# One-core HGRN2, stick-breaking attention and PEER experts: how the experts' input is repeated, and which block moves are transposes

## The chip, the cores and the metric

The kernel runs on one core of one Trainium2 chip. The time is device microseconds of one execution. Of the kernel before there are three runs, 3661.49, 3661.97 and 3666.92 us, median 3661.97, and one more execution under the profiler, which took 3659.19 us.

## The reference, cut to what matters

A model of two layers over 1024 tokens of 1024 features, all in float32. Layer 0 mixes tokens with HGRN2, layer 1 with stick-breaking attention; each layer then has a PEER stage, in which every token reads 64 experts out of 16384.

```python
# layer l: mix, then experts
hn = modulate(rms_norm(h, norm_mix_g[l]), sh1, sc1)
mix = hgrn2_mixer(...) if l == 0 else stick_breaking_mixer(...)
h = h + g1 * mix
hn = modulate(rms_norm(h, norm_ffn_g[l]), sh2, sc2)
h = h + g2 * peer_ffn(hn, ...)

# stick-breaking attention, per query block: a key counts only if it is earlier
mask = s_pos < t_pos
log_keep = where(mask, log_sigmoid(-z), 0)
a = where(mask, exp(z + cs_in + after), 0)      # then a @ v

# experts, per token: 4 heads x 16 best of 128 x 128 keys
hid = einsum('cd,ced->ce', x, u[experts])
w = gates * gelu(hid)
out = einsum('ce,ced->cd', w, v[experts])
```

## The kernel before, in words

**Blocks and stages.** The 1024 tokens are eight blocks of 128. Layer 0's mixer runs on three groups of blocks (`G0`: 0-1, 2-4, 5-7), `hgrn_group`, each followed by its routing (`mix_route`), which finds the 64 experts of each token. Layer 1's attention runs on two groups (`G1`: 0-3, 4-7), `attn_group`, each followed by `route_group`. The attention of a group needs layer 0 finished for the group's blocks, and the experts of a block need its routing. So the expert stage of one set of blocks runs beside the mixer of the next.

**The expert stage.** Each row of a table holds an expert's `u` and `v` (2048 floats). A block is worked off in four quarters of 32 tokens (`peer_quarter`). A quarter's 32 tokens stand on the 128 partitions four times, one copy per head, so that one gather (`L690`, an indirect DMA issued by GpSimd, 128 rows of 8 KB, 1 MB) brings one expert for each token and head, and 16 gathers make a quarter. VectorE multiplies the `u` half with the tokens' input `hq` and sums along the row (`L692`), ScalarE takes gelu of the sums of two gathers (`L694`) and scales a small selection matrix with them (`L696`, tile `sel`), and TensorE adds up the `v` halves, weighted, in PSUM (`L699`, tile `va`; four matmuls per gather, each two instructions in the profile, since a float32 matmul is made of two). The gather tile `g` has six buffers; a buffer is free once L699 has read it.

**The experts' input.** `peer_input` makes the block's normed and modulated tokens `hn2` (128 x 1024, one buffer). Its modulation rows come from columns: `row_bcast` (`L183`) multiplies a column, repeated 128 times as the stationary operand, with the identity, which gives the column as a row on all partitions. `peer_rep` repeats a quarter: two matmuls (`L666`) with a 0/1 matrix `rep4` take the 32 partitions of the quarter in `hn2` to four places, in two halves of 512 columns through one PSUM bank (tag `pq`, one buffer), and ScalarE copies each half to `hq` (`L667`, two buffers). It also makes `dg` (`L669`), the gates on diagonals, with `delta`, a part of `rep4`.

**Other block moves.** `norm_T` (`L266`) turns normed token blocks so that features stand on partitions, by matmul with the identity, or with the reversed identity `anti` where attention wants the keys in reverse. `norm_heads` (`L423`) makes rows of the head norms as `row_bcast` does. Two places already use TensorE's transpose mode: `L502` and `L783`.

**The attention head.** `attn_head` multiplies queries and keys into PSUM, up to four key blocks at a time (`L770`); for the diagonal block a second matmul (`L772`) adds `amask`, -1e30 where the key is not earlier. ScalarE takes tanh (`L773`, tile `th`), VectorE forms the stick-breaking weights with a running product (`L774` to `L777`), TensorE turns them (`L783`), ScalarE copies them (`L784`), TensorE multiplies with the values (`L786`).

**What sets the order.** The Tile framework orders the instructions of each engine when the kernel is built, by a list scheduler with its own estimates of durations. `at(t)` gives what follows a due time: the gathers of block b in layer l are due at `T0 + PERIOD * (8l + b + i/64) - LEAD`, a quarter's repeat (`peer_rep`) 20 before its first gather, which is about six gathers, and the first quarter's 60. Each engine then works off its queue in that fixed order, waiting by semaphores.

Of the kernel before, what the change touches and what calls it, by code (L numbers as in the profile page):

```python
# [10 lines left out]
F32 = mybir.dt.float32  # L11
BF16 = mybir.dt.bfloat16
I32 = mybir.dt.int32
U32 = mybir.dt.uint32
AF = mybir.ActivationFunctionType
ALU = mybir.AluOpType
# [6 lines left out]
GH, GMAX = 3, 4  # L23
# [2 lines left out]
FREE = 1  # L26
LEAD, RLEAD = 100, 60
NC = 2
BIG = -1e30
NEG = -3.0e38  # L30

T0, PERIOD = 305.0, 207.0
# [5 lines left out]
def tile_model(ctx, tc, x, cin, small, ada, w_in, w_out, kvada, kvw, sbq, sbo, wq, subk, tab0, tab1, out):  # L38
    nc = tc.nc
    V, S, G, T = nc.vector, nc.scalar, nc.gpsimd, nc.tensor  # L40

    cp = ctx.enter_context(tc.tile_pool(name="cp", bufs=1))
# [9 lines left out]
    def unit(tag, shape=(128, 1024)):  # L52
        seq[0] += 1
        return bp.tile(list(shape), F32, tag=tag, name=f"{tag}_{seq[0]}", bufs=BUFS[tag])
# [23 lines left out]
    def at(t):  # L78
        tc.cur_priority = int(20 * t) + 10

    def sm(tag, shape, dt=F32, bufs=2):
        seq[0] += 1
        return sp.tile(list(shape), dt, tag=tag, name=f"{tag}_{seq[0]}", bufs=bufs)

    def bank(tag="ps"):
        seq[0] += 1
        return pp.tile([128, 512], F32, tag=tag, name=f"{tag}_{seq[0]}", bufs=PBUFS[tag])
# [33 lines left out]
    ident = cp.tile([128, 128], F32, name="ident")  # L121
    make_identity(nc, ident)
    anti = cp.tile([128, 128], F32, name="anti")
# [6 lines left out]
    iota16 = cp.tile([128, 16], F32, name="iota16")  # L130
    G.iota(iota16, pattern=[[1, 16]], base=0, channel_multiplier=0, allow_small_or_imprecise_dtypes=True)

    amask = cp.tile([128, 128], F32, name="amask")
    G.memset(amask, 0.0)
    G.affine_select(out=amask, in_=amask, compare_op=ALU.is_gt, fill=BIG, base=-127, pattern=[[1, 128]], channel_multiplier=1)
    start = cp.tile([128, GH * 8, 16], BF16, name="start")
    G.memset(start, 0.0)
    G.memset(start[:, :, 0:1], 1.0)

    rep4 = cp.tile([128, 4, 32], F32, name="rep4")  # L140
    G.memset(rep4, 0.0)
    for i in range(4):
        G.affine_select(out=rep4, in_=rep4, compare_op=ALU.not_equal, fill=1.0, base=-32 * i, pattern=[[0, 4], [-1, 32]], channel_multiplier=1)
    delta = rep4[:, 0, :]


    def zero_where(t, pattern, base, cm, op):
        G.affine_select(out=t, in_=t, compare_op=op, fill=0.0, base=base, pattern=pattern, channel_multiplier=cm)

    mk = []  # L150
    for lvl in range(3):
        m = sm("qr", [128, 128 * GMAX], bufs=1)[:, 0:128]
        G.memset(m, 1.0)
        if lvl == 0:
            zero_where(m, [[1, 128]], 0, -1, ALU.is_ge)
            v3 = m.rearrange("p (c j) -> p c j", j=16)
            zero_where(v3, [[-16, 8], [0, 16]], 0, 1, ALU.is_ge)
        else:
            B = 16 << (lvl - 1)
            v3 = m.rearrange("p (c two j) -> p c two j", two=2, j=B)  # L160
            G.memset(v3[:, :, 0, :], 0.0)
            z = v3[:, :, 1, :]
            n = 128 // (2 * B)
            zero_where(z, [[-2 * B, n], [0, B]], 0, 1, ALU.is_ge)
            zero_where(z, [[2 * B, n], [0, B]], B - 1, -1, ALU.is_ge)
        mi = cp.tile([128, 128], I32, name=f"mk{lvl}")
        V.tensor_copy(mi, m)
        mk.append(mi)
    NSC = 2
    scTs = []  # L170
    for i in range(NSC):
        t = cp.tile([128, 128], F32, name=f"scT{i}")
# [6 lines left out]
    def row_bcast(col, k0, n, tag):  # L179

        ps = bank(tag)
        for k in range(n):
            T.matmul(ps[:, 128 * k:128 * k + 128], lhsT=col[:, k0 + k:k0 + k + 1].to_broadcast([128, 128]), rhs=ident, start=True, stop=True)  # L183
        return ps

    S.activation(trow, crow, AF.Tanh, scale=0.5)
# [2 lines left out]
    for half in range(2):  # L189
        c = slice(512 * half, 512 * half + 512)  # L190
        ps = bank()
# [69 lines left out]
    def norm_T(hs, dst, scale, shift, rev=False):  # L261
        for half in range(2):
            ps = bank()
            for j in range(4):
                k = 4 * half + j
                T.matmul(ps[:, 128 * j:128 * j + 128], lhsT=hs[:, 128 * k:128 * k + 128], rhs=anti if rev else ident, start=True, stop=True)  # L266
            for j in range(4):
                k = 4 * half + j
                src = ps[:, 128 * j:128 * j + 128]
                if j % 2:  # L270
                    last["norm"] = S.activation(dst[:, k, :], src, AF.Identity, scale=scale[:, k:k + 1], bias=shift[:, k:k + 1]).ins
                else:
                    V.tensor_scalar(out=dst[:, k, :], in0=src, scalar1=scale[:, k:k + 1], scalar2=shift[:, k:k + 1], op0=ALU.mult, op1=ALU.add)  # L273

    def blk(i):
        return slice(128 * i, 128 * i + 128)

    def mix_row(l, half):
        g = unit("gs", (128, 512))
        S.copy(g, row_bcast(modc[l], 16 + 4 * half, 4, "ps"))  # L280
        return g
# [134 lines left out]
    def norm_heads(n, half, oT, r8):  # L416
        r = r8[:, 0:n, 4 * half:4 * half + 4]
        V.tensor_scalar(out=r, in0=r, scalar1=1.0 / 128, scalar2=EPS, op0=ALU.mult, op1=ALU.add)
        G.tensor_tensor(out=r, in0=r, in1=nhalf[:, 0:n, 0:4], op=ALU.pow)
        for i in range(n):  # L420
            ps = bank()
            for j in range(4):
                T.matmul(ps[:, blk(j)], lhsT=r8[:, i, 4 * half + j:4 * half + j + 1].to_broadcast([128, 128]), rhs=ident, start=True, stop=True)  # L423
            o = oT[:, 4 * half:4 * half + 4, blk(i)]
            last["tail"] = V.tensor_tensor(out=o, in0=o, in1=ps.rearrange("p (a t) -> p a t", a=4), op=ALU.mult).ins

    def hgrn_head(n, hd, hT, oT, r8, tags):
# [78 lines left out]
        for i in range(n):  # L506
# [7 lines left out]
            T.matmul(ps[0:64, 384:448], lhsT=k2[:, c0], rhs=q2[:, c1], start=True, stop=True)  # L514
            sT = scTs[sc_i[0] % NSC]
            sc_i[0] += 1
# [105 lines left out]
    def quarter_rows(col):  # L622

        t = sm("bg", [128, 256], bufs=1)
        for k in (0, 4):
            ps = row_bcast(col, k, 4, "pq")
            for c in (k // 2, k // 2 + 1):
                p = slice(32 * c, 32 * c + 32)
                S.copy(t[p, :], ps[p, 256 * (c % 2):256 * (c % 2) + 256])
        return t  # L630
# [17 lines left out]
    def pos(l, b, i):  # L648
        return T0 + PERIOD * (8 * l + b + i / 64) - LEAD
# [8 lines left out]
    def peer_rep(l, b, q):  # L658

        at(pos(l, b, 16 * q) - (20 if q else RLEAD))  # L660
        hn2 = hn2s[l, b]
        p = slice(32 * q, 32 * q + 32)
        t = unit("hq")
        for k in range(2):
            ps = bank("pq")
            T.matmul(ps, lhsT=rep4[p].rearrange("p j u -> p (j u)"), rhs=hn2[p, 512 * k:512 * k + 512], start=True, stop=True)  # L666
            S.copy(t[:, 512 * k:512 * k + 512], ps)  # L667
        dg = sm("dg", [128, 16, 32])
        V.tensor_tensor(out=dg, in0=delta[:, None, :].to_broadcast([128, 16, 32]), in1=idx[l, b][1][:, q, :, None].to_broadcast([128, 16, 32]), op=ALU.mult)  # L669
        hqs[l, b, q] = t, dg  # L670
        if b == q == 0:
            gates[l] = quarter_rows(modc[l][:, 40:48])
# [89 lines left out]
    def attn_head(b, qT, kh, vh, th, st):  # L762
        n = b + 1
        L = 128 * n
        for h0 in range(0, n, 4):
            m = min(4, n - h0)
            ps = bank("pj")
            i0 = 7 - b + h0
            o = ps[:, 0:128 * m]
            T.matmul(o, lhsT=qT, rhs=kh[:, i0:i0 + m, :].rearrange("p a t -> p (a t)"), start=True, stop=(h0 > 0))  # L770
            if h0 == 0:
                T.matmul(ps[:, 0:128], lhsT=ident, rhs=amask, start=False, stop=True)  # L772
            S.activation(th[:, 128 * h0:128 * (h0 + m)], o, AF.Tanh, scale=0.5 / math.sqrt(128.0))  # L773
        V.memset(st[:, 0:1], 1.0)  # L774
        V.tensor_scalar(out=st[:, 1:L], in0=th[:, 0:L - 1], scalar1=-0.5, scalar2=0.5, op0=ALU.mult, op1=ALU.add)
        V.tensor_tensor_scan(out=st[:, 1:L], data0=st[:, 1:L], data1=ones[:, 0:1].to_broadcast([128, L - 1]), initial=1.0, op0=ALU.mult, op1=ALU.mult)
        V.scalar_tensor_tensor(th[:, :L], th[:, :L], 1.0, st[:, :L], op0=ALU.add, op1=ALU.mult)  # L777
        po = bank("po")
        for h0 in range(0, n, 4):
            m = min(4, n - h0)  # L780
            ps = bank()
            for j in range(m):
                T.transpose(ps[:, blk(j)], th[:, blk(h0 + j)], ident)  # L783
            S.copy(st[:, 128 * h0:128 * (h0 + m)], ps[:, 0:128 * m])  # L784
        for j in range(n):
            T.matmul(po[:, 0:128], lhsT=vh[:, 7 - b + j, :], rhs=st[:, blk(j)], start=(j == 0), stop=(j == n - 1))  # L786
        S.activation(qT, po[:, 0:128], AF.Copy, scale=0.5)
# [30 lines left out]
    t = unit("g", (128, 2048))  # L818
# [81 lines left out]
```

## Time and profile before

| | |
|---|---|
| median of three runs | 3661.97 us (3661.49 to 3666.92) |
| profiled execution | 3659.19 us, span 3657.5 us |
| granted TensorE clock, mean | 0.824 |
| TensorE busy | 2820.3 us (77%), 19940 instructions |
| VectorE busy | 2488.9 us (68%) |
| GpSimd busy | 1519.8 us (42%) |
| ScalarE busy | 1019.6 us (28%) |
| DMA | 1272.97 MB, mean 348 GB/s; the gathers 1073.81 MB |

A share of busy time is a mean over all stages. The engines' names in the profile are PE (TensorE matmul), PEld (its weight loads, which overlap with PE), DVE (VectorE), ACT (ScalarE), POOL (GpSimd) and SP (the DMA queue of the sync engine). `L666` is line 666 of the kernel. The granted clock is a share of full speed: 1.0 is 2.4 GHz, 0.5 is 1.2 GHz, and a mean between is time at either. The chain of waits is followed back from the last instruction, at each step to what released it; its shares add up to the stretch it is asked for.

### The profile page before, as it was taken

Reading aid. Unit: us, or ns where it says so; the run is one execution under the profiler, and the core shown is the slowest. Engines: PE = TensorE matmul, PEld = TensorE weight load, DVE = VectorE, ACT = ScalarE, POOL = GpSimd, SP = SyncE. Lnnn points to the kernel's source line nnn. Section 1 sums busy time; section 2 is a strip of 40 time slices with the busy share of each in tenths; the row PEclk is TensorE's granted clock in tenths of the full one; section 3 lists DMA queues with packets and bytes.
Section 4 is the critical chain, followed back from the end, with each engine's and each line's share of the span. In section 5 each row is a group of like instructions: output and inputs, shape, how many; then the busy total and the mean of one; then the engine's idle time right before and its main releaser. Section 6 shows DMA issues by size and latency. Waiting matters only on the chain.

```text
span 3657.5 us, 54482 instructions
## 1 busy us (share of the span) xinstructions
PE 2820.3 (77%) x19940; PEld 1782.4 (49%) x19940; DVE 2488.9 (68%) x5732; ACT 1019.6 (28%) x3071; POOL 1519.8 (42%) x1682
## 2 busy tenths in 40 slices
PE   5898999988999989999944589888898445454443
PEld 4787666775667745668411235555573111111111
DVE  7858767599765886655798546666657975555554
ACT  2114222233221333332322223332332222222221
POOL 3322665345653333333334433343433344444443
PEclk8898999999998999999955589999999555555555
DMA  9944988888988889999999998888898999999998
GB/s 395 345 178 176 339 343 340 340 337 310 355 340 338 331 321 364 351 346 361 352 342 358 409 361 347 334 343 326 338 368 331 337 384 411 404 407 412 393 412 342
DMA packets 203882, 1272.97 MB, mean 348 GB/s; under 512 B 22625, under 2 KB 22753, under 8 KB 72546
## 3 DMA queue, kind: packets, MB, share of 16 engines
q0 software_dynamic: 147456, 1073.81, 74.8%
q1 hardware_dynamic: 56162, 195.69, 14.1%
q8 instruction: 160, 2.62, 0.3%
q14 instruction: 104, 0.85, 0.1%
HBM read 1261.02 MB, written 8.39 MB: 347 GB/s over the span
## 4 chain that ended last, share of the span: by engine, by line
PE 45%; DVE 22%; issue 14%; DMA 9%; POOL 7%; ACT 3%; POOLq 0%; SPq 0%; DVEq 0%; ACTq 0%
DMA g<-in_tab_dram,ev 9%; DVE g L692 7%; PE pj L441 7%; PE va L699 7%; POOL g L690 6%; PE pj L749 3%; PE pj L732 3%; PE pj L753 3%; PE ps L358 3%; PE ps L295 3%; PE pq L666 2%; PE pj L445 2%; PE po L786 2%; DVE g L214 2%; PE pj L548 1%
## 5 line engine op out<-in xcount | busy, mean ns | idle before, releaser
L690 POOL DMA_INDIRECT g<-in_tab_dram,ev x1024 | 1208.4, 1180 | 1790.2 <-PE va L699 1245.7
L692 DVE SCALAR_TENSOR_TENSOR g<-g,hq 128x1024 f32<-128x1024 f32 x1024 | 1269.5, 1245 | 526.6 <-DMA g<-in_tab_dram,ev 489.1
L699 PE MATMUL va<-g,sel 128*32 128x256 f32 x8192 | 741.5, 491 | 527.9 <-ACT sel L696 527.4
L699 PEld LDWEIGHTS va<-g,sel 128*32 128x32 f32 x8192 | 251.4, 130 | 981.0 <-ACT sel L696 748.5
L694 ACT ACTIVATE w<-hid 128x2 f32<-128x2 f32 x512 | 104.4, 204 | 1350.2 <-DVE g L692 1326.7
L441 PE MATMUL pj<-T,wt 128*128 128x384 f32 (+1 forms) x1152 | 361.1, 462 | 0.0
L666 PE MATMUL pq<-hn,rep 32*128 32x512 f32 x256 | 190.6, 832 | 115.0 <-ACT hq L667 101.6
L696 ACT ACTIVATE sel<-dg,w 128x32 f32<-128x32 f32 x1024 | 273.3, 314 | 14.1
L441 PEld LDWEIGHTS pj<-T,wt 128*128 128x128 f32 x1152 | 214.8, 194 | 105.3 <-issue 11.1
L490 POOL TENSOR_TENSOR K<-K,F 128x384 f32<-128x384 f32 (+1 forms) x144 | 148.6, 1056 | 68.2 <-DVE T L462 40.6
L214 DVE SCALAR_TENSOR_TENSOR g<-g,vr 128x1024 f32<-128x1024 f32 x104 | 131.1, 1286 | 6.6 <-DMA g<-in_ada_dram 6.4
L753 PEld LDWEIGHTS pj<-wt,T 128*128 128x128 f32 x1024 | 122.0, 192 | 23.1 <-issue 21.0
L666 PEld LDWEIGHTS pq<-hn,rep 32*128 32x128 f32 x256 | 47.5, 230 | 175.3 <-ACT hq L667 128.1
L753 PE MATMUL pj<-wt,T 128*128 128x128 f32 x1024 | 132.0, 279 | 0.0
L445 PE MATMUL pj<-wt,T 128*128 128x128 f32 x1024 | 129.0, 278 | 0.0
L445 PEld LDWEIGHTS pj<-wt,T 128*128 128x128 f32 x1024 | 120.9, 192 | 12.5 <-issue 6.4
L295 PE MATMUL ps<-wt,T 128*128 128x128 f32 x1024 | 121.9, 277 | 0.0
L295 PEld LDWEIGHTS ps<-wt,T 128*128 128x128 f32 x1024 | 116.7, 192 | 10.2 <-issue 9.3
L548 PE MATMUL pj<-T,wt 128*128 128x512 f32 x256 | 115.7, 598 | 0.0
L732 PE MATMUL pj<-T,wt 128*128 128x512 f32 x256 | 115.6, 601 | 0.0
L266 PE MATMUL ps<-ident,K 128*128 128x128 f32 x480 | 79.4, 325 | 46.4 <-ACT K L255 29.2
L749 PE MATMUL pj<-T,wt 128*128 128x512 f32 x256 | 114.7, 594 | 0.5 <-DVE T L273 0.5
(240 smaller groups left out, 4204.3 us busy)
## 6 DMA issues: line engine op xcount, KB each, us to landing
wt<-in_w_in_dram SPq DMA_DIRECT2D x96, 512.0 KB
g<-in_ada_dram SPq DMA_DIRECT2D x88, 512.0 KB
g<-in_tab_dram,ev POOLq DMA_INDIRECT x1024
wt<-in_kvw_dram SPq DMA_DIRECT2D x32, 512.0 KB
wt<-in_w_out_dram SPq DMA_DIRECT2D x18, 512.0 KB
wt<-in_wq_dram SPq DMA_DIRECT2D x17, 512.0 KB
g<-in_kvada_dram SPq DMA_DIRECT2D x16, 512.0 KB
wt<-in_sbq_dram SPq DMA_DIRECT2D x16, 512.0 KB
```

The source lines that it names most:

```text
L214: V.scalar_tensor_tensor(w, w, 1.0, act_c, op0=ALU.mult, op1=ALU.mult, accum_out=acc[:, g:g + 1])
L295: T.matmul(ps[:, blk(c)], lhsT=oT[:, k, blk(i)], rhs=ws[c][:, k, :], start=(k == 0), stop=(k == 7))
L441: T.matmul(pw, lhsT=w[:, k, :], rhs=hT[:, k, 0:W], start=(k == 0), stop=(k == 7))
L445: T.matmul(ps[:, blk(i)], lhsT=hT[:, k, blk(i)], rhs=w[:, k, :], start=(k == 0), stop=(k == 7))
L666: T.matmul(ps, lhsT=rep4[p].rearrange("p j u -> p (j u)"), rhs=hn2[p, 512 * k:512 * k + 512], start=True, stop=True)
L690: G.indirect_dma_start(out=t, out_offset=None, in_=tab, in_offset=bass.IndirectOffsetOnAxis(ap=ev[:, q, c + k:c + k + 1], axis=0))
L692: V.scalar_tensor_tensor(u, u, 1.0, hq, op0=ALU.mult, op1=ALU.mult, accum_out=hid[:, k:k + 1])
L696: S.activation(sel[:, k, :], dg[:, c + k, :], AF.Copy, scale=wt[:, k:k + 1])
L699: T.matmul(va[32 * m:32 * m + 32, 0:256], lhsT=sel[:, k, :], rhs=ts[k][:, 1024 + 256 * m:1280 + 256 * m], start=(c + k == 0), stop=(c + k ...
L732: T.matmul(ps[:, 0:W], lhsT=w[:, k, :], rhs=hT[:, k, 0:W], start=(k == 0), stop=(k == 7))
L749: T.matmul(ps[:, 0:W], lhsT=w[:, k, :], rhs=hT[:, k, 0:W], start=(k == 0), stop=(k == 7))
L753: T.matmul(ps[:, blk(i)], lhsT=hT[:, k, blk(i)], rhs=w[:, k, :], start=(k == 0), stop=(k == 7))
```

## The change

Three things are done. `peer_rep` fills `hq` by four ScalarE copies of 32 partitions from `hn2`, one to each quarter of the partitions, in place of two matmuls through PSUM and two copies; `rep4` is gone and `delta` stands alone. The row broadcasts (`row_bcast`, `norm_heads`) and the forward case of `norm_T` use TensorE's transpose mode; the reversed case stays a matmul. In the attention head the matmul with `amask` is gone; after tanh VectorE sets the diagonal block's entries to -1 by a predicated copy, with `amask` now an integer mask that is made beside the other masks.

```diff
--- before.py
+++ after.py
@@ -26,7 +26,6 @@
 FREE = 1
 LEAD, RLEAD = 100, 60
 NC = 2
-BIG = -1e30
 NEG = -3.0e38
 
 T0, PERIOD = 305.0, 207.0
@@ -130,18 +129,17 @@
     iota16 = cp.tile([128, 16], F32, name="iota16")
     G.iota(iota16, pattern=[[1, 16]], base=0, channel_multiplier=0, allow_small_or_imprecise_dtypes=True)
 
-    amask = cp.tile([128, 128], F32, name="amask")
-    G.memset(amask, 0.0)
-    G.affine_select(out=amask, in_=amask, compare_op=ALU.is_gt, fill=BIG, base=-127, pattern=[[1, 128]], channel_multiplier=1)
+    amask = cp.tile([128, 128], I32, name="amask")
+    neg = cp.tile([128, 1], F32, name="neg")
+    G.memset(neg, -1.0)
     start = cp.tile([128, GH * 8, 16], BF16, name="start")
     G.memset(start, 0.0)
     G.memset(start[:, :, 0:1], 1.0)
 
-    rep4 = cp.tile([128, 4, 32], F32, name="rep4")
-    G.memset(rep4, 0.0)
+    delta = cp.tile([128, 32], F32, name="delta")
+    G.memset(delta, 0.0)
     for i in range(4):
-        G.affine_select(out=rep4, in_=rep4, compare_op=ALU.not_equal, fill=1.0, base=-32 * i, pattern=[[0, 4], [-1, 32]], channel_multiplier=1)
-    delta = rep4[:, 0, :]
+        G.affine_select(out=delta, in_=delta, compare_op=ALU.not_equal, fill=1.0, base=-32 * i, pattern=[[-1, 32]], channel_multiplier=1)
 
 
     def zero_where(t, pattern, base, cm, op):
@@ -166,6 +164,10 @@
         mi = cp.tile([128, 128], I32, name=f"mk{lvl}")
         V.tensor_copy(mi, m)
         mk.append(mi)
+    m = sm("qr", [128, 128 * GMAX], bufs=1)[:, 0:128]
+    G.memset(m, 0.0)
+    G.affine_select(out=m, in_=m, compare_op=ALU.is_gt, fill=1.0, base=-127, pattern=[[1, 128]], channel_multiplier=1)
+    V.tensor_copy(amask, m)
     NSC = 2
     scTs = []
     for i in range(NSC):
@@ -180,7 +182,7 @@
 
         ps = bank(tag)
         for k in range(n):
-            T.matmul(ps[:, 128 * k:128 * k + 128], lhsT=col[:, k0 + k:k0 + k + 1].to_broadcast([128, 128]), rhs=ident, start=True, stop=True)
+            T.transpose(ps[:, 128 * k:128 * k + 128], col[:, k0 + k:k0 + k + 1].to_broadcast([128, 128]), ident)
         return ps
 
     S.activation(trow, crow, AF.Tanh, scale=0.5)
@@ -263,7 +265,10 @@
             ps = bank()
             for j in range(4):
                 k = 4 * half + j
-                T.matmul(ps[:, 128 * j:128 * j + 128], lhsT=hs[:, 128 * k:128 * k + 128], rhs=anti if rev else ident, start=True, stop=True)
+                if rev:
+                    T.matmul(ps[:, 128 * j:128 * j + 128], lhsT=hs[:, 128 * k:128 * k + 128], rhs=anti, start=True, stop=True)
+                else:
+                    T.transpose(ps[:, 128 * j:128 * j + 128], hs[:, 128 * k:128 * k + 128], ident)
             for j in range(4):
                 k = 4 * half + j
                 src = ps[:, 128 * j:128 * j + 128]
@@ -420,7 +425,7 @@
         for i in range(n):
             ps = bank()
             for j in range(4):
-                T.matmul(ps[:, blk(j)], lhsT=r8[:, i, 4 * half + j:4 * half + j + 1].to_broadcast([128, 128]), rhs=ident, start=True, stop=True)
+                T.transpose(ps[:, blk(j)], r8[:, i, 4 * half + j:4 * half + j + 1].to_broadcast([128, 128]), ident)
             o = oT[:, 4 * half:4 * half + 4, blk(i)]
             last["tail"] = V.tensor_tensor(out=o, in0=o, in1=ps.rearrange("p (a t) -> p a t", a=4), op=ALU.mult).ins
 
@@ -659,12 +664,9 @@
 
         at(pos(l, b, 16 * q) - (20 if q else RLEAD))
         hn2 = hn2s[l, b]
-        p = slice(32 * q, 32 * q + 32)
         t = unit("hq")
-        for k in range(2):
-            ps = bank("pq")
-            T.matmul(ps, lhsT=rep4[p].rearrange("p j u -> p (j u)"), rhs=hn2[p, 512 * k:512 * k + 512], start=True, stop=True)
-            S.copy(t[:, 512 * k:512 * k + 512], ps)
+        for j in range(4):
+            S.copy(t[32 * j:32 * j + 32, :], hn2[32 * q:32 * q + 32, :])
         dg = sm("dg", [128, 16, 32])
         V.tensor_tensor(out=dg, in0=delta[:, None, :].to_broadcast([128, 16, 32]), in1=idx[l, b][1][:, q, :, None].to_broadcast([128, 16, 32]), op=ALU.mult)
         hqs[l, b, q] = t, dg
@@ -767,10 +769,9 @@
             ps = bank("pj")
             i0 = 7 - b + h0
             o = ps[:, 0:128 * m]
-            T.matmul(o, lhsT=qT, rhs=kh[:, i0:i0 + m, :].rearrange("p a t -> p (a t)"), start=True, stop=(h0 > 0))
-            if h0 == 0:
-                T.matmul(ps[:, 0:128], lhsT=ident, rhs=amask, start=False, stop=True)
+            T.matmul(o, lhsT=qT, rhs=kh[:, i0:i0 + m, :].rearrange("p a t -> p (a t)"), start=True, stop=True)
             S.activation(th[:, 128 * h0:128 * (h0 + m)], o, AF.Tanh, scale=0.5 / math.sqrt(128.0))
+        V.copy_predicated(th[:, 0:128], amask, neg.to_broadcast([128, 128]))
         V.memset(st[:, 0:1], 1.0)
         V.tensor_scalar(out=st[:, 1:L], in0=th[:, 0:L - 1], scalar1=-0.5, scalar2=0.5, op0=ALU.mult, op1=ALU.add)
         V.tensor_tensor_scan(out=st[:, 1:L], data0=st[:, 1:L], data1=ones[:, 0:1].to_broadcast([128, L - 1]), initial=1.0, op0=ALU.mult, op1=ALU.mult)
```

## Rows read from the trace of the kernel before

**Rows 1.** Windows: busy PE, PEld, DVE, ACT, POOL; granted clock, DMA share, GB/s.
```profile
300.00:1200.00 900.00, 851.11 (x6128) 608.75 (x6127) 677.73 (x1597) 259.98 (x775) 452.21 (x597) 0.95 0.85 325
...
1200.00:1800.00 600.00, 562.42 (x4100) 376.78 (x4099) 406.78 (x1067) 210.16 (x626) 211.47 (x200) 0.97 0.90 347
...
2130.00:2800.00 670.00, 601.24 (x4213) 380.94 (x4210) 407.28 (x690) 217.26 (x644) 251.39 (x214) 0.97 0.87 339
...
3000.00:3657.00 657.00, 306.91 (x2246) 101.32 (x2246) 338.42 (x554) 137.60 (x481) 285.27 (x258) 0.53 0.98 398
...
1100.00:1200.00 100.00, 94.62 (x767) 76.94 (x767) 57.57 (x103) 20.94 (x67) 41.20 (x50) 0.88 0.89 339
```

**Rows 2.** Chain by line: 0-300, 300-1200, 1200-1800, 2130-2800, 3000-3657 us.
```profile
by line: DVE g L214 19.4%; PE pj L441 15.7%; PE ps L358 8.6%; DVE K L452 3.4%; DMA h<-in_x_dram 3.4%; DMA h<-in_ada_dram 3.4%; POOL K L490 2.9%; PE ps L423 2.5%; PE pj L445 2.4%; DVE scT L518 2.2%; PE po L520 2.0%; DMA g<-in_ada_dram 1.9%; 
...
by line: PE pj L441 22.2%; PE va L699 9.2%; PE ps L358 8.2%; DVE g L692 7.2%; PE pj L445 7.0%; issue 4.8%; PE pq L666 2.6%; DMA g<-in_tab_dram,ev 2.5%; PE pj L391 2.0%; DVE K L452 1.6%; PE ps L423 1.5%; PE pq L183 1.5%; PE ps L523 1.4%; PE 
...
by line: PE va L699 11.9%; PE pj L753 10.0%; PE pj L749 9.2%; PE pj L732 8.3%; PE ps L295 7.5%; PE pj L548 7.3%; issue 6.2%; PE pj L391 4.3%; DVE g L692 3.6%; POOL g L690 3.5%; PE po L786 3.4%; PE pq L666 3.3%; PE pj L770 2.1%; DMA g<-in_ta
...
by line: PE va L699 9.5%; PE pj L732 8.5%; PE pj L749 8.3%; PE ps L295 7.8%; PE po L786 7.3%; DMA g<-in_tab_dram,ev 7.1%; DVE K L776 6.8%; PE pj L753 6.8%; DVE g L692 5.6%; issue 5.3%; PE ps L783 3.5%; PE pq L666 3.0%; PE ps L266 2.3%; PE p
...
by line: issue 43.3%; DMA g<-in_tab_dram,ev 26.4%; POOL g L690 19.7%; DVE g L692 3.7%; PE va L699 1.7%; PE pq L183 1.3%; POOLq L690 0.7%; PE pq L666 0.6%; ACT sel L696 0.5%; DVE hn L641 0.4%; DVE h L705 0.4%; ACT w L694 0.3%; POOL rstd_out 
```

**Rows 3.** TensorE groups, 300-1800 us: form, count | busy, mean ns | idle before, releaser.
```profile
L699 PE MATMUL va<-g,sel 128*32 128x256 f32 x3184 | 228.3, 402 | 19.9 <-ACT sel L696 19.6
...
L266 PE MATMUL ps<-anti,K 128*128 128x128 f32 x64 | 8.5, 281 | 1.6 <-ACT T L271 1.6
```

**Rows 4.** TensorE groups by shape, 2130 to 2800 us.
```profile
L699 PE MATMUL va<-g,sel 128*32 128x256 f32 x1540 | 109.7, 402 | 21.8 <-ACT sel L696 21.8
...
L266 PE MATMUL ps<-anti,K 128*128 128x128 f32 x64 | 8.8, 283 | 2.0 <-ACT T L271 1.7 <-issue 0.3
```

**Rows 5.** Sums over 300-1800 and 2130-2800 us: L666, L183, L266, L423, L772.
```profile
sum 2170.00, PE 94.19 PEld 24.32; mean PE 47.10 PEld 12.16
...
sum 2170.00, PE 55.30 PEld 48.66; mean PE 27.65 PEld 24.33
...
sum 2170.00, PE 83.04 PEld 75.21; mean PE 41.52 PEld 37.60
...
sum 2170.00, PE 17.35 PEld 16.29; mean PE 8.68 PEld 8.15
...
sum 2170.00, PE 24.86 PEld 23.93; mean PE 12.43 PEld 11.96
```

**Rows 6.** Groups by shape, whole span, ScalarE and VectorE.
```profile
L667 ACT COPY hq<-pq 128x512 f32<-128x512 f32 x128 | 74.4, 582 | 128.6 <-PE pq L666 80.7 <-DVE g L692 47.3
...
L702 ACT COPY vr<-va 32x256 f32<-32x256 f32 x256 | 93.0, 363 | 31.4 <-DVE va L700 24.1 <-DVE g L692 2.3 <-DVE K L777 1.9
...
L245 ACT ACTIVATE K<-h 128x1024 f32<-128x1024 f32 x30 | 31.6, 1054 | 47.0 <-DMA h<-in_x_dram 20.0 <-DVE h L298 12.0 <-DVE h L361 6.7
...
L518 DVE COPY_PREDICATED scT<-mk,ps 128x128 f32<-128x128 int32 x192 | 56.5, 294 | 30.0 <-PE ps L514 26.1 <-PE ps L512 0.9 <-issue 0.7
```

**Rows 7.** Timeline of TensorE (start, duration): bursts of block moves.
```profile
953.70 1.14 PE L183 MATMUL pq<-ident,modc 128*128 128x128 f32 x8
...
1536.55 0.60 PE L783 MATMUL ps<-ident,K 128*128 128x128 f32 x4
...
2624.92 1.63 PE L783 MATMUL ps<-ident,K 128*128 128x128 f32 x7
```

**Rows 8.** Timeline, GpSimd's gather issues and VectorE's products, steady stretch.
```profile
3215.94 1.25 POOL L690 DMA_INDIRECT g<-in_tab_dram,ev  x1 [3.72 <-PE va L699]
...
3220.91 1.25 POOL L690 DMA_INDIRECT g<-in_tab_dram,ev  x1 [2.48 <-PE va L699]
...
3225.10 1.22 DVE L692 SCALAR_TENSOR_TENSOR g<-g,hq 128x1024 f32<-128x1024 f32 x1 [1.25 <-DMA g<-in_tab_dram,ev]
...
3227.59 1.22 DVE L692 SCALAR_TENSOR_TENSOR g<-g,hq 128x1024 f32<-128x1024 f32 x1 [1.26 <-DMA g<-in_tab_dram,ev]
```

## The prediction

> **What bounds the kernel now.** I read the windows first, stage by stage, since the page's busy shares mix stages with different limits. The reader is to see two kinds of stretch. From 300 to 1800 us and from 2130 to 2800 us TensorE is busy 90 to 95% at a granted clock of 0.95 to 0.97, while DMA stands at 0.85 to 0.90 [rows 1]. From 3000 us to the end DMA is at 0.98, TensorE at 47% and at half speed, 0.53 (the 1.2 GHz level) [rows 1]. I call them TensorE-led and DMA-led. The stretches between (1800 to 2130, 2800 to 3000) are routing, where VectorE and DMA share the lead.
>
> Second I read the chain of waits stage by stage. In the TensorE-led stretches its largest parts are matmul lines (L441, L699, L753, L749, L732), and the repeat matmul L666 has 2.6%, 3.3% and 3.0% of them; at the end it is issue, gathers' DMA and GpSimd's issues, with 0.6% for L666 [rows 2]. So a microsecond taken from TensorE can shorten the first kind of stretch and hardly the second.
>
> Third, how tight the gather loop is. In 300 to 1800 us the expert matmuls L699 stood idle for their weights `sel` only 19.9 us, in 2130 to 2800 us 21.8 us [rows 3, 4]: ScalarE is ahead of TensorE there. In a steady DMA-led stretch the gather issued at 3215.94 is multiplied at 3225.10, 9.2 us later, and the gather behind it at 3227.59, 2.5 us after that. When the next gather is issued at 3220.91, DMA has work until 3227.59; less the issue's own 1.25 us, some 5 us of queue cover a late release [rows 8].
>
> **The change part by part.** Terms are against the profiled execution, 3659.2 us (span 3657.5 and 1.7 around it); the median of the runs shown, 3662.0, is 2.8 above.
>
> *TensorE work removed in the TensorE-led stretches.* L666 goes whole: 94.2 us [rows 5]. Row broadcasts (L183), forward block transposes (L266) and head-norm rows (L423) go from two passes per block to one. Four blocks as matmuls (x8) take 1.14 us, four as transposes (x4, L783) 0.60 us, so 0.48 of their time goes [rows 7]. L183: 55.3 x 0.48 = 26.5. L266: 83.0 less the reversed ones that stay (8.5 + 8.8 [rows 3, 4]) = 65.7 x 0.48 = 31.5. L423: 17.4 x 0.48 = 8.3. The mask matmul L772 goes whole: 24.9. Sum 185 us of 2170 [rows 5].
>
> How much of it lies on the path: L666's chain shares are 2.6% of 900, 3.3% of 600 and 3.0% of 670 us, together 63 us [rows 2], two thirds of its 94. At the same share, 125 of the 185 us are on the chain. What is late next there is the gather loop and VectorE: VectorE is busy 61 to 75%, DMA 0.85 to 0.90 against 0.98 at the end [rows 1], and the order of work is fixed per engine, so part of the relief waits for them. Ends: nothing comes back (0), or all of the 125. I take three fifths, 75 us: VectorE leads in about a quarter of these stretches (the routing of blocks), and some is lost in the fixed order.
>
> *First 300 us.* L423 has 2.5% of the chain, 7.5 us [rows 2]; 0.48 of it is 4 us less. GpSimd's set-up swaps one mask for another and narrows four selects; the loads of x and of the first modulation weights, 6.8% of the chain there [rows 2], cover it, so nothing is counted.
>
> *ScalarE's copies.* Per quarter two 128x512 copies at 582 ns go, four 32x1024 copies come. No row shows that copy. A 32x256 copy takes 363 ns, and 512 columns 582, so 0.855 ns a column: 1024 columns come to 1.02 us; the 128x1024 square from SBUF takes 1.054 [rows 6]. These are the ends; I take 1.04, between them. Four are 4.16, less 1.16: 3.0 us more per quarter, 192 us over 64. ScalarE is busy 29 to 35% in the TensorE-led stretches [rows 1], so the cover is its idle time. Queued behind a copy on ScalarE are the gelu and `sel` of the next gather pair, the head masks' copies and the projections' PSUM evacuations; TensorE waits for those, and GpSimd's next gather for TensorE. The copies are due some six gathers ahead of the quarter that reads them, so the planner can put them between `sel` pairs; one pair then meets at most one copy. The TensorE-led stretches hold (3184 + 1540)/128 = 37 quarters (8 matmul instructions per gather, 16 gathers) [rows 3, 4]. At 0.4 us each they cost 15 us. Ends: nothing, or the block of four that the rival below prices. In the other 27 quarters the 5 us of queued DMA hides a 4.2 us block: nothing counted. If that cover were gone, each would cost up to its 3 us more.
>
> *Waits that go.* hq no longer passes a PSUM bank, so TensorE's queue no longer stops for that bank between the two halves. Late in the kernel, where these stops are, DMA leads: nothing counted. hn2 is released by copies and not by matmuls, a few us later, within the six gathers of lead.
>
> *The mask.* 64 copies by predicate on VectorE. From PSUM one takes 294 ns [rows 6]; 64 are 19 us, all between 1200 and 2800 us. The mask runs after tanh, before the head's scan, on the chain where the scan L776 is (6.8% of 2130 to 2800 [rows 2]). A quarter of it on the path: 5 us. Ends 0 and 19.
>
> *A rule against the transposes.* Transposes at L783 took 0.15 us apiece in a burst (4 in 0.60) and 0.23 (7 in 1.63) at another moment [rows 7]; the run has no stretch with transposes alone, so it does not show what they do to the granted clock. The Trainium skill, page "TensorE: Matmul & The Clock Gate", section "Part 4: PE-mode transpose", says that transposes don't count as TensorE activity in the way matmuls do, so the full clock does not engage for them; no run here shows that. By the rows alone the sum stands; by the rule the granted clock would fall where transposes replace matmuls, and that is the fourth rival.
>
> *Sum.* -75 - 4 + 15 + 5 = -59: 3600 for the profiled execution, 3603 on the median's footing.
>
> **The rivals.**
> 1. *ScalarE's copies become the wait; slower.* If the four copies stand in a block, a `sel` pair behind it comes 4.2 us late. L699 hardly waits for `sel` now [rows 3, 4], so some 1.5 us of lead absorbs part; 2.7 us x 37 = 100 us. -75 - 4 + 100 + 5 = +26: 3688. It decides once a pair's delay passes its lead in the TensorE-led stretches, or 5 us in the DMA-led. For it: fixed queues. Against: ScalarE's idle time.
> 2. *The relief finds the gather loop.* A fifth of the 125 returns: -25 - 4 + 10 + 5 = -14, 3648. For it: the chain holds VectorE's product, 7.2%, and gathers' DMA, 2.5 to 7.1%, in the same stretches [rows 2]. Against: TensorE at 95%.
> 3. *All on the chain returns.* ScalarE's cost 5: -125 - 4 + 5 + 5 = -119, 3543. For it: DMA at 0.87 leaves room up to 0.98 [rows 1], some 240 us of 2170. Against: the routing stretches.
> 4. *The clock falls under transposes.* If the TensorE-led stretches fell from 0.96 to the 0.88 that 1100 to 1200 us had [rows 1], their 2015 us of TensorE, less 185, would stretch by 0.96/0.88 to 1996: 19 us relieved and not 185. On the path two thirds of three fifths, 7.5: -7.5 - 4 + 15 + 5 = +8.5, 3670. Against: matmuls surround the bursts.
>
> The planner also works out a new order of the queues; that is in each case's spread, some 20 us to either side.
>
> **How the numbers follow.** Forecast 0.42, rivals 0.15, 0.24, 0.13 and 0.06. I predict the likeliest, 3603; its own range is 3570 to 3640. The range of 8 in 10 reaches to rival 3's centre and rival 1's: 3545 to 3685. A measurement of this kernel tells 0.2%, 7 us, from no change: faster is below 3655. Faster: 0.41 of the forecast, 0.17 of rival 2, 0.13 of rival 3, 0.01 of rival 4: 0.72. Same: 0.01, 0.05, 0.02 of these and 0.01 of rival 1: 0.09. Slower: 0.14 of rival 1, 0.02 of rival 2, 0.03 of rival 4: 0.19.
>
> **What would show it.** Right: L666 and L772 are gone; L183, L266 and L423 show one instruction per block, some 0.15 us each in a burst; the copies are near 1.04 us, 256 of them; the stretch up to the end of the head group at 1200 us and both attention stretches shrink, together by some 75 us, with DMA's share up towards 0.90 there; the last 650 us stay. Wrong: L699's idle time on `sel` in the TensorE-led stretches grows from 42 us to 100 or more (rival 1); the stretches keep their length with TensorE's busy share down near 85% (rival 2); the granted clock there falls below 0.92 (rival 4); or the time goes into the last stretch, with DMA's share under 0.95 and gathers waiting for the copies.

## The result and the profile after

The changed kernel took 3684.05 us (median of four runs, 3680.17 to 3693.60) against 3661.73 us before: a ratio of 1.0068, 95% interval 1.0041 to 1.0095. It is slower; I had forecast 3603, faster. The profiled execution took 3693.6 us, 9.6 above its median, so its stretches are read for their shape and the ratio for the size.

The windows of the changed kernel, in the columns of [rows 1] (busy PE, PEld, DVE, ACT, POOL, then granted clock, DMA share, GB/s):

```profile
300.00:1200.00 900.00, 809.54 (x6102) 589.73 (x6102) 685.28 (x1641) 309.88 (x823) 457.54 (x601) 0.95 0.86 334
1200.00:1800.00 600.00, 523.74 (x3657) 338.13 (x3656) 416.58 (x1109) 241.87 (x637) 200.03 (x194) 0.92 0.89 339
...
2130.00:2800.00 670.00, 570.10 (x3949) 365.70 (x3952) 409.46 (x700) 247.32 (x648) 241.86 (x207) 0.92 0.86 334
...
3000.00:3692.00 692.00, 253.51 (x2156) 83.59 (x2156) 343.54 (x561) 181.89 (x512) 297.52 (x262) 0.51 0.95 384
```

Against [rows 1], TensorE is busy 42, 39 and 31 us less in the three TensorE-led windows, 111 of the 185 us that I had counted on; the clock in the second and third is 0.92 where it was 0.97, and DMA's share hardly moves. In the last window DMA stood at 0.98 and has fallen to 0.95. Windows of fixed times can't show whether a stretch has become shorter, so I count the gathers in order of issue. The 257th (the fifth block's first) starts at 1262 us against 1288: up to here the change is ahead by 26 us. The 769th (the 13th block's first) starts at 2980 against 2972, and the last at 3666 against 3631: of the 35 us between the two profiled executions, 26 are lost in the last quarter of the gathers, and the lead of 26 is lost before it with 8 more.

The operations themselves, by line and shape (count | busy us, mean ns | idle before):

```profile
L669 ACT COPY hq<-hn 32x1024 f32<-32x1024 f32 x256 | 266.8, 1042 | 38.8 <-DVE g L694 35.4
...
L185 PE MATMUL pq<-ident,modc 128*128 128x128 f32 x272 | 54.2, 333 | 26.3 <-DVE gt L616 10.4 <-DVE hn L646 6.6 <-DVE hn L645 6.0
...
L774 DVE COPY_PREDICATED_SCALAR K<-amask,neg 128x128 f32 x64 | 22.8, 357 | 66.0 <-ACT K L773 50.5 <-ACT K L785 11.2 <-PE va L701 4.1
```

The copy takes the 1.04 us that I took; the broadcasts are one instruction per block; the mask's copy is 0.36 us where I had 0.29. The durations are not what failed. Where the copies stand is: along ScalarE's queue the four of a quarter are back to back in all 64 quarters, and in 46 of them they stand directly between a gelu (L696) and the `sel` (L698) that follows from it. They also stand earlier than their due time: the block starts when some 12 gathers before the quarter's first have still to be issued, twice the six that `at` asks for. A quarter's change in the last stretch, by engine (start, duration):

```profile
3244.19 1.27 POOL L692 DMA_INDIRECT g<-in_tab_dram,ev  x1 [2.46 <-PE va L701]
...
3245.76 0.94 POOL L692 DMA_INDIRECT g<-in_tab_dram,ev  x1 [0.30 <-issue]
...
3247.17 0.20 ACT L696 ACTIVATE w<-hid 128x2 f32<-128x2 f32 x1 [4.21 <-DVE g L694]
3247.40 4.20 ACT L669 COPY hq<-hn 32x1024 f32<-32x1024 f32 x4
...
3251.62 0.53 ACT L698 ACTIVATE sel<-dg,w 128x32 f32<-128x32 f32 x2
3252.00 1.94 PE L701 MATMUL va<-g,sel 128*32 128x256 f32 x16 [7.26 <-ACT sel L698]
...
3252.19 0.69 DVE L671 TENSOR_TENSOR dg<-delta,gt 128x512 f32<-128x512 f32 x1 [2.56 <-ACT sel L698]
3252.80 1.22 DVE L694 SCALAR_TENSOR_TENSOR g<-g,hq 128x1024 f32<-128x1024 f32 x1
...
3254.34 0.97 POOL L692 DMA_INDIRECT g<-in_tab_dram,ev  x1 [0.27 <-DVE g L694]
```

Windows of 1 us there, in the columns of [rows 1]:

```profile
3253.00:3254.00 1.00, 0.94 (x12) 0.05 (x4) 1.00 (x2) 0.20 (x2) 0.71 (x1) 0.50 0.87 360
3254.00:3255.00 1.00, 0.33 (x4) 0.20 (x8) 0.43 (x3) 0.88 (x4) 0.73 (x2) 0.50 0.14 57
3255.00:3256.00 1.00, 1.00 (x16) 0.40 (x8) 0.06 (x1) 0.97 (x4) 0.88 (x2) 0.50 0.00 0
3256.00:3257.00 1.00, 0.77 (x9) 0.20 (x2) 1.00 (x2) 0.34 (x1) 0.92 (x1) 0.50 0.92 188
```

The reader is to see one chain. The gelu is done at 3247.4, its `sel` only starts at 3251.6. TensorE, which reads `sel`, has idled 7.3 us, where 3.1 were usual just before. VectorE's `dg` reuses the buffer that this `sel` reads, so it waits too, and the product of a gather that has landed waits behind `dg`. No buffer comes free, and GpSimd issues no gather from 3245.76 to 3254.34, 8.6 us where a pair was issued every 5.0. What was queued is nearly all in by 3254, and the next gather, issued at 3254.34, begins to move only after 3256: between them the queue has run dry, and DMA moves next to nothing for 2 us.

### The profile page after: what moved, and what is told of

It reads as the page before. It is cut to its first block, busy times and chain, and to the rows that moved or that the text cites. A ratio compares the mean times of both kernels' runs of the same rounds, so it can differ in the third digit from the quotient of the medians.

```text
span 3691.9 us, 52706 instructions
## 1 busy us (share of the span) xinstructions
PE 2589.1 (70%) x18916; PEld 1656.2 (45%) x18916; DVE 2506.7 (68%) x5797; ACT 1217.6 (33%) x3199; POOL 1536.4 (42%) x1683
## 4 chain that ended last, share of the span: by engine, by line
PE 36%; DVE 24%; issue 16%; DMA 12%; POOL 7%; ACT 6%; POOLq 0%; SPq 0%; DVEq 0%; another core or an unknown queue 0%; ACTq 0%
DMA g<-in_tab_dram,ev 11%; DVE g L694 8%; PE pj L446 6%; POOL g L692 5%; PE va L701 5%; PE pj L751 3%; PE ps L300 2%; PE pj L553 2%; ACT hq L669 2%; PE pj L755 2%; PE pj L450 2%; PE po L787 2%; PE pj L734 2%; PE ps L363 1%; DVE K L777 1%
## 5 line engine op out<-in xcount | busy, mean ns | idle before, releaser
L701 PE MATMUL va<-g,sel 128*32 128x256 f32 x8192 | 758.1, 503 | 805.5 <-ACT sel L698 803.8
L701 PEld LDWEIGHTS va<-g,sel 128*32 128x32 f32 x8192 | 259.0, 133 | 1226.8 <-ACT sel L698 1045.5
L696 ACT ACTIVATE w<-hid 128x2 f32<-128x2 f32 x512 | 104.4, 204 | 1266.9 <-DVE g L694 1243.8
L669 ACT COPY hq<-hn 32x1024 f32<-32x1024 f32 x256 | 266.8, 1042 | 38.8 <-DVE g L694 35.4
L698 ACT ACTIVATE sel<-dg,w 128x32 f32<-128x32 f32 x1024 | 273.0, 314 | 15.4
L787 PE MATMUL po<-K 128*128 128x128 f32 x576 | 105.9, 333 | 16.8 <-ACT K L785 16.7
L787 PEld LDWEIGHTS po<-K 128*128 128x128 f32 x576 | 92.8, 235 | 52.1 <-ACT K L785 27.9
```

Of the source, the lines that this page charges most:

```text
L669: S.copy(t[32 * j:32 * j + 32, :], hn2[32 * q:32 * q + 32, :])
L698: S.activation(sel[:, k, :], dg[:, c + k, :], AF.Copy, scale=wt[:, k:k + 1])
L701: T.matmul(va[32 * m:32 * m + 32, 0:256], lhsT=sel[:, k, :], rhs=ts[k][:, 1024 + 256 * m:1280 + 256 * m], start=(c + k == 0), stop=(c + k ...
```

## The experiments

My theory after the result was that place, not amount, is what costs; its rivals were the amount of ScalarE work, a clock that falls under transposes, and the mask on the attention head's chain. Ratios are against the kernel before, run beside; its median was 3651 to 3662 us from round to round, so differences between experiments are taken from the ratios. "Last stretch" is from the 769th gather's start to the last one's in the one profiled execution (before: 659 us, changed: 685). Four kernels that repeat by matmuls have 654 to 659 there, so I read nothing into differences below 5 us. Each edit also lets the planner order the other instructions anew, so each ratio includes what that order does.

**The parts alone.** The matmul repeat put back into the changed kernel:

```diff
...
-        for j in range(4):
-            S.copy(t[32 * j:32 * j + 32, :], hn2[32 * q:32 * q + 32, :])
+        for k in range(2):
+            ps = bank("pq")
+            T.matmul(ps, lhsT=rep4[p]..., rhs=hn2[p, 512 * k:512 * k + 512], start=True, stop=True)
+            S.copy(t[:, 512 * k:512 * k + 512], ps)
```

> The changed kernel with the experts' input repeated by two matmuls again; transposes and mask as changed. Copies theory (four copies of 1.04 us stand in one block between a gelu and its sel, and hold back the gather loop): the loss goes, the last stretch returns to 659 us from the 13th block's first gather to the last, and what transposes and mask give remains: 3630 to 3655. Clock theory (transposes let the granted clock fall): the clock between 1200 and 1800 us stays near 0.92 as in the changed kernel and the time stays at 3665 or more. Mask theory (the predicated copy lengthens the attention head's chain): blocks 4 to 6 of layer 0 still lose some 25 us, 3665 or more.

Measured 0.9969 (0.9953 to 0.9984), 3650.27 us, last stretch 658 us, the clock between 1200 and 1800 us 0.95: the loss goes.

The four copies alone in the kernel before (that edit the other way round):

> The kernel before with ScalarE's four copies alone; matmul broadcasts and the mask matmul stay. Copies theory: slower than the changed kernel or as slow, 3680 to 3710, the last stretch some 27 us longer, TensorE's idle time on sel up by 250 us or more over the whole span. Clock theory: the clock between 1200 and 1800 us stays at 0.97 and the time is 3640 to 3665.

Measured 1.0085 (1.0065 to 1.0105), last stretch 686 us, TensorE's idle time on `sel` over the whole span 778 us against 528. The clock between 1200 and 1800 us was 0.96, between 2130 and 2800 us 0.92. The copies are the loss, and more than all of it.

Transposes alone (`T.matmul(..., rhs=ident)` to `T.transpose(..., ident)` in `row_bcast`, `norm_T`, `norm_heads`):

> The kernel before with transposes in place of the broadcast and forward block matmuls, nothing else. Copies theory: faster, 3630 to 3655, granted clock between 1200 and 1800 us 0.95 to 0.97. Clock theory: not faster, 3660 or more, clock near 0.92.

Measured 0.9977 (0.9963 to 0.9990), 3653.38 us, clock 0.95: a small gain, 8 us. In the profiled execution the 257th gather is 22 us ahead of the kernel before (1266 against 1288) and the 769th 4 (2967 against 2972): most of what is gained early is given back in between.

The mask alone (L772's matmul out, `V.copy_predicated(th[:, 0:128], amask, ...)` behind the tanh):

> The kernel before with the diagonal mask set by VectorE behind the tanh, nothing else: 64 pairs of mask matmul instructions (25 us of TensorE in the TensorE-led stretches) against 64 predicated copies of 0.36 us (23 us of VectorE). Copies theory: within 10 us of before. Mask theory: slower by 15 to 30 us, all of it between 1260 and 1800 us and between 2130 and 2800 us.

Measured 1.0009 (0.9996 to 1.0023), last stretch 654 us: no difference that can be told. The parts multiply to 1.0071, the change gave 1.0068: they add up.

**Place or amount.** The same block of four, queued behind the `sel`:

```diff
...
+        with after("sel"):
             for j in range(4):
                 S.copy(t[32 * j:32 * j + 32, :], hn2[32 * q:32 * q + 32, :])
```

> The changed kernel with the four copies queued behind the last sel of the quarter before, still as one block of 4.2 us. Place theory (what costs is that the block stands between a gelu and its sel): in the steady DMA-led stretch ScalarE has 4.2 us between a sel and the next gelu, so the last stretch (13th block's first gather to the last gather) returns from 686 us to 655 to 665 and the time to 3635 to 3655, as with the matmul repeat or better. Amount theory (192 us more of ScalarE cost, wherever they stand): 3675 or more, last stretch 680 or more.

Measured 0.9948 (0.9928 to 0.9968), 3632.03 us, last stretch 657 us. The same work is 44 us apart by the ratios (1.0068 against 0.9948), 28 of them in the last stretch (685 against 657), with the block behind the `sel` in place of before it. On the footing of the first runs 0.9948 is 3643 us, inside the place theory's range.

One copy behind the `sel` of each pair; the copies wait in a list, `pend`:

```diff
...
             for k in range(NC):
-                S.activation(sel[:, k, :], ...)
+                last["sel"] = S.activation(sel[:, k, :], ...).ins
+            if pend and c >= 4:
+                with after("sel"):
+                    S.copy(*pend.pop(0))
```

> The changed kernel with the four copies of a quarter spread, one behind the sel of each pair from the third pair on. Place theory: no pair meets a block; last stretch 655 to 660 us, DMA share from 3000 to 3600 us back to 1.00, time 3630 to 3650. Amount theory: 3675 or more.

Measured 0.9909 (0.9890 to 0.9928), 3617.24 us, last stretch 645 us, DMA share 1.00 from 3000 to 3600 us (it was 1.00 before the change too). This version beats both kernels, and by more than I had expected: the last stretch is 10 us shorter than the 655 that I gave as its least. ScalarE in it, in order of time:

```profile
3252.66 0.53 ACT L702 ACTIVATE sel<-dg,w 128x32 f32<-128x32 f32 x2
3253.22 1.04 ACT L705 COPY hq<-hn 32x1024 f32<-32x1024 f32 x1
3257.45 0.20 ACT L700 ACTIVATE w<-hid 128x2 f32<-128x2 f32 x1 [3.19 <-DVE g L698]
3257.69 0.53 ACT L702 ACTIVATE sel<-dg,w 128x32 f32<-128x32 f32 x2
```

Each copy fits in the time in which ScalarE waits for the next products; after it 3.2 us of idle time are left.

The spread copies in the kernel before, without transposes and mask:

> The kernel before with the four ScalarE copies spread, one behind the sel of a pair; no transposes, mask matmul kept. Against it stands the run with the planner's block of four (1.0085 of before). Place theory: the same 192 us of ScalarE work cost next to nothing and the repeat matmuls' 191 us of TensorE are gained in part: 0.991 to 0.997 of before. Amount theory: 1.004 or more.

Measured 0.9928 (0.9910 to 0.9947), last stretch 645 us. Block against spread, 1.0085 against 0.9928: 57 us for the same instructions.

The four copies on VectorE (`V.tensor_copy`):

> The changed kernel with the same four copies on VectorE. VectorE's predicated copies of 128 columns take 0.36 us; a plain copy of 1024 columns is bounded by 0.5 and 1.25 us, so 2 to 5 us a quarter, in VectorE's queue before the next quarter's products. Place theory: sel is no longer held, the product is; the last stretch takes 660 to 685 us by the copy's length, 3640 to 3685. Amount theory: the amount moves to an engine that is busy 61 to 75% in the TensorE-led stretches, 3690 or more.

Measured 0.9971 (0.9958 to 0.9984). The copy took 0.71 us, 2.8 us a quarter in VectorE's queue, last stretch 654 us, shorter than the 660 to 685 that I had; the time is inside its range.

**The length of the block**, where the planner puts it (`for j in range(2)` with 64 partitions; 32, 32 and 64; a single `S.copy(t, hn2)`):

> The changed kernel with two copies of 64 partitions per quarter in place of four of 32 (half of the repeat is left out: the copies take the wrong tokens for some heads, so the result is not the reference's). A block of 2.1 us, half the amount, the planner's place. Place theory with some cover by queued gathers: well under half of the loss stays, 3650 to 3662. Amount theory: half of the loss, 3664 to 3672.

> The changed kernel with three copies per quarter, a block of 3.1 us where the planner puts it (the tokens don't stand on the right partitions). Straight-line theory: half way between two copies and four, 1.000 of before. Cover theory: nearer to two copies, 0.993 to 0.997, with the DMA share between 3000 and 3600 us at 0.99 or 1.00.

> The changed kernel with one copy of 128 partitions per quarter where the planner puts it, a block of 1.04 us (three quarters of the repeat are left out: the tokens don't stand on the right partitions). Cover theory (a block between gelu and sel costs only what goes beyond the queued gathers' cover): as the spread copies, 0.989 to 0.993 of before. Straight-line theory (each microsecond in front of sel costs the same): with 1.0068 at 4.2 us and 0.993 at 2.1 us, 0.986.

| copies | block | ratio | last stretch |
|---|---|---|---|
| 1 | 1.0 us | 0.9903 (0.9886 to 0.9920) | 647 us |
| 2 | 2.1 us | 0.9930 (0.9912 to 0.9949) | 657 us |
| 3 | 3.1 us | 1.0038 (1.0024 to 1.0052) | 674 us |
| 4 | 4.2 us | 1.0068 (1.0041 to 1.0095) | 685 us |

One copy met the cover theory's number. Two were faster than either theory had it (0.9930 is 3636 us on the footing of the first runs), and three met neither number. In the last stretch the first microsecond is free (647 us against 645 with spread copies), and each copy after it costs 10 to 17 us over the 15 blocks of copies there: 0.7 to 1.1 us a block for 1.04 us more, on average nearly in full. Between two and three copies nothing else changes there: from the 777th gather on, TensorE, VectorE and GpSimd work in the same order, and ScalarE too but for the copy that is added. With fewer copies layer 1 gathers other experts, as many and as large. Over the whole time the step from two to three is larger than its neighbours; most of it lies before the last stretch (the 769th gather starts at 2946 us with two, at 2972 with three), where the order of other work changes too; why, I have not settled.

**Is TensorE the limit where it is 90% busy?** Half of the contraction left out in the projections, on the spread version (`for k in range(8)` to `range(4)`, `stop=(k == 3)`):

> The changed kernel with spread copies and half of the contraction left out in the HGRN, query, key and value projections (four of eight steps), about 400 us of TensorE less in the TensorE-led stretches; all loads stay. TensorE-led theory as predicted (two thirds on the chain, three fifths of that returned): 150 us or more below the spread copies, 3470 or less. Loop theory (gathers, VectorE and the fixed order already limit those stretches): less than 80 us below, 3540 or more, with the DMA share there still under 0.93.

Measured 0.9751 (0.9733 to 0.9769), 3560.41 us, by the ratios 58 us below the spread version. Its windows:

```profile
300.00:1200.00 900.00, 708.68 (x5572) 513.19 (x5572) 747.59 (x1953) 339.49 (x888) 453.54 (x608) 0.88 0.87 335
1200.00:1800.00 600.00, 430.71 (x3104) 253.97 (x3104) 416.87 (x1083) 230.47 (x601) 214.97 (x200) 0.80 0.93 358
2130.00:2800.00 670.00, 472.19 (x3480) 291.70 (x3480) 505.36 (x1178) 257.40 (x660) 259.26 (x217) 0.80 0.88 335
```

TensorE's busy time over the span is 306 us less (2584.1 to 2278.5) at a lower clock, DMA's share hardly higher, VectorE at 75 to 83% in two of the three. The half that is gone took 429 us at the spread version's durations; what is left runs at the lower clock, hence the 306. So a microsecond taken from TensorE returned 0.13 us, or 0.19 of the net relief, and in the profiled executions 12 us of the gain come before the first gather (308 us against 321). This is other and more TensorE work than the change took away, so it is a guide and not the change's own price.

## Why the prediction was wrong, step by step

1. **The step that failed: "the planner can put them between `sel` pairs; one pair then meets at most one copy"**, 15 us. The lead of six gathers makes a copy due, it does not spread it. The buffer of `hq` (there are two) comes free with the last product of the quarter that is just ending, which is also what the gelu waits for, so all four become ready there and went as one block, mostly ahead of the `sel`, when 12 gathers and not six were still to be issued before the quarter. Block against spread is 58 us (1.0068 against 0.9909). The spread version is the kernel that the forecast described, one copy per pair: it came to -33 us where the sum had -59. The result is +25 by its ratio, so of 84 us between it and the sum 58 are the block and 26 the relief (point 3).
2. **"In the other 27 quarters the 5 us of queued DMA hides a 4.2 us block: nothing counted."** Measured 40 us in the last stretch alone (685 against 645), the larger part of the 58. I had subtracted only the issue's 1.25 us from the queued work. What a new gather needs with nothing ahead of it stood in the trace of before: the first gather is issued at 335.0, its product starts at 341.2.

```profile
L690 POOL DMA_INDIRECT g<-in_tab_dram,ev x1024: 932/980/2972, 335.0 to 3631.0; - x171
...
L692 DVE SCALAR_TENSOR_TENSOR g<-g,hq x1024: 1160/1219/5356, 341.2 to 3641.3; 128x1024 f32<-128x1024 f32 x171
```

   (Both are groups of the kernel before: least, median and longest in ns, first and last start.) A lone gather takes 6.2 us, a queued one 9.2 [rows 8], so the cover is at most the 3 us between them. The gather issued into the dry queue at 3254.34 in the changed kernel agrees: its product starts at 3260.52, 6.2 us later. The cost begins sooner, between one copy and two; that `dg` and the quarter's own work take the rest of the cover is my reading and not tested.
3. **"I take three fifths, 75 us"** of 185, 0.40 per microsecond. The half contraction returned 0.13, about rival 2's price (a fifth of 125, of 185). Transposes and mask together gave 11 us (0.9969). The spread copies alone gave 26 us, 14 of them in the last stretch. The chain's shares say where the path runs now, not what is next; VectorE, the gather loop's latency and the clock were close behind. Which of them leads in those stretches stays open.
4. **"Late in the kernel, where these stops are, DMA leads: nothing counted."** Wrong to the other side: with spread copies the last stretch is 645 us, with the matmul repeat 654 to 659. In the kernel before 46 of the 128 copies of L667 also stand directly between a gelu and its `sel`, and ScalarE waited 80.7 us for L666 there [rows 6]; that this is what cost those 9 to 14 us is likely and not tested by itself.
5. **The mask**, +5 us: measured 0.9996 to 1.0023, consistent with it. **The first 300 us**, -4: the first gather starts at 323 in place of 335, a larger gain than counted and a small term.

Rival 1 named the mechanism and gave 3688 against 3684 measured, but that match is luck: it had 100 us for the block, all in the TensorE-led stretches and none at the end, where the block cost 58 in all and 40 of them at the end, and it set against them a relief of 75 us that did not come. It had "fixed queues" for it and got 0.15; that the four copies become ready at one instant, together with the gelu, could be read from the code and was the argument missing.

Of the signs that I had named, rival 1's did not reach its mark: the idle time of the expert matmuls on `sel` in the TensorE-led windows went from 42 us [rows 3, 4] to 81 and not to 100. It is a poor sign, since the spread version, the fastest that leaves nothing out, has 112 us there. The changed kernel's two windows first, then the spread version's (idle before, behind the last bar):

```profile
L701 PE MATMUL va<-g,sel 128*32 128x256 f32 x3200 | 240.5, 420 | 55.2 <-ACT sel L698 54.0 <-ACT w L696 0.9
L701 PE MATMUL va<-g,sel 128*32 128x256 f32 x1524 | 108.9, 406 | 26.2 <-ACT sel L698 25.7 <-issue 0.4
...
L708 PE MATMUL va<-g,sel 128*32 128x256 f32 x3264 | 240.5, 412 | 61.3 <-ACT sel L702 60.7
L708 PE MATMUL va<-g,sel 128*32 128x256 f32 x1532 | 109.6, 407 | 50.2 <-ACT sel L702 50.0
```

Rival 2's sign did appear (TensorE busy 90, 87 and 85%), and so did a loss in the last stretch with DMA's share down to 0.95. Rival 4's was a clock below 0.92; 0.95, 0.92 and 0.92 came to its edge, and that was not the cause: the spread version has 0.95, 0.92 and 0.91. The clock fell also where only TensorE's work was less: 0.92 from 2130 to 2800 us with copies and no transposes, 0.88 to 0.80 with half of the contraction. With spread copies and no transposes it was 0.97, 0.96 and 0.94; the transposes also take work off TensorE, so whether they add to the fall is open.

## What to carry to other kernels

Ask of an instruction that is moved to an idle engine not how busy the engine is, but at which instant it becomes ready and what stands behind it in that queue then: here the list scheduler placed it at that instant, and what stood between a producer and its consumer on the critical loop cost, beyond the first microsecond, nearly its full length at every turn. Price the cover of a DMA queue as at most the queued latency less the latency of a lone transfer. Before counting on relief of the busiest engine, ask what the same stretch does with much less of its work; here less than a fifth came back.

## What the runs showed of the hardware that I had not expected

A ScalarE copy of 32 partitions x 1024 columns, to the same or another quarter of the partitions, takes 1.042 us on average, as long as an operation on 128 partitions of that width (1.054 [rows 6]); VectorE took 0.71 us for it. The predicated copy with a repeated scalar took 0.357 us, against 0.294 for one from PSUM [rows 6].
